# A hybrid decoder step on one core: 64-column chunk-loop weights, spread samples, the two projections one after the other

## The chip, the cores and the metric

One Trainium2 chip, and of it one core with its engines: TensorE (PE; its weight loads are listed as PEld), VectorE (DVE), ScalarE (ACT), GpSimd (POOL) and SyncE (SP), which issues most transfers. The metric is the device time of one execution in microseconds. A kernel's time is the median of its runs.

## The reference

One trunk layer on 512 new tokens of a prompt and 8 single tokens of other sequences, 520 columns in all, of width 2048. A shared RMS norm feeds one wide input projection. From it come a recurrent branch (RWKV-7, 16 heads of 64, with a state of 64 x 64 per head) and a convolution branch (31 taps, a layer norm), each with a gate and a projection to 2048. Two sigmoid gates merge them; an output projection, a per-layer embedding with its own gate, and a final RMS norm follow.

```python
def step(S, inp):
    r_t, w_t, k_t, v_t, a_t, b_t = inp
    sa = jnp.einsum('bhij,bhj->bhi', S, a_t)
    S = S * w_t[:, :, None, :] + sa[..., None] * b_t[:, :, None, :] + v_t[..., None] * k_t[:, :, None, :]
    return S, jnp.einsum('bhij,bhj->bhi', S, r_t)
...
o = ((o - mu) * lax.rsqrt(var + GN_EPS)).reshape(Bn, T, D_A) * lnx_g + lnx_b
...
y_a = jnp.einsum('btc,cd->btd', (o * jax.nn.silu(gate_a.astype(f32))).astype(dt), w_proj_a)
...
cb = jax.nn.silu(cf) * jax.nn.silu(gate_b.astype(f32))
y_b = jnp.einsum('btc,cd->btd', cb.astype(dt), w_proj_b)
m = jax.nn.sigmoid(ga) * y_a + jax.nn.sigmoid(gb) * y_b
h = x + jnp.einsum('btd,de->bte', m, w_out)
```

## The kernel before

The activations lie with channels on the 128 partitions and the 520 tokens along the row. Every large product is done in three passes on split operands: each weight block is split into a high and a low part (`wh` on ScalarE, `wl` on VectorE, both from `split`), the activations likewise, and `step` (L153) issues the six multiplications of one 128 x 128 weight block, three passes by two halves of 260 columns, all recorded as L165. `gemm` (L169) calls `step` 8 or 16 times for one output tile, and after each step calls `tick`.

`tick` (L143) is what interleaves the work. All small work is written as Python generators; each step of a large product advances every generator by one, and `yield n` makes a generator skip n steps. So the `yield` numbers set how many large products stand between two pieces of small work in TensorE's queue, whose order is the order of the program. The queues of the other engines are put in order by the scheduler of the compiler, from the same dependences; each engine runs its queue strictly in order. There are 2224 steps in all.

The main loop (in `rest`'s neighbour at the end of the first stage) runs eight rounds p, one for each pair of heads, with nine products of 16 steps each: k, r, v, the first gate, two for the convolution's gated input, its gate and two of the 32 merge gates, 144 steps a round. Beside it run generators:

- `wkv` (L358): the recurrent branch of round p, one round behind. It makes decays and keys, the column sums `bv` (two multiplications at L257/L258, a few steps after `yield 8`), and the chunk matrices (L446). A 32-row triangular inverse follows on VectorE, a multiplication `tm` and a reduction `ti` (L484) per row, in chunk form for eight chunks of 64 tokens. Then come the transposes of the values (L526) and keys (L538), and the chunk loop (L546 to L574): for each chunk a product with the state columns `suv` (L549), the mask product with `nbr` of the chunk before (L551), a copy `xs`, the product with the inverse `ttb` (L556), copies of its result into `suv` (one on VectorE L557, one on ScalarE L558, and `xu` on POOL L561), the product that updates the state (L564), and on VectorE the update of `suv` (L568) and `sf` (L571). Between these three places are `ly` steps, 4 in most rounds, and 7 in the last. The outputs go through a group norm on VectorE, then, 16 steps later, eight pairs of 64 x 64 transposes (L595, L596), a scale and shift `og`, and two multiplications on POOL.
- `conv` (L621): 30 multiply-adds on VectorE, three steps apart.
- `samples` and `sample` (L658, L678): the single tokens' state update, eight blocks, each four multiplications on POOL and three multiplications or sums and two reductions on VectorE of 128 x 512. They start 12 steps into the last round's generator `rest`.
- `lnorm` (L715): the convolution's layer norm, from `csum`, with the tiles read back from memory; `reload` (L769) brings the recurrent branch's output back as `ya`.

When the rounds and the remaining merge gates are done, the generators are drained, `yb` is split, and for each of 16 output tiles the two projections follow each other, `gemm(8, ya)` and `gemm(8, yb)`, each multiplied by its gate. The output product and the per-layer gate follow; `finish` (L904) does the final norm for each half of the tokens, with multiplications on POOL and VectorE named by `ON_POOL` and written out in `GROUPS`.

## Time and profile before

| | |
|---|---|
| median of 3 runs | 1880.88 us |
| lowest, highest | 1878.25, 1882.21 us |
| profiled execution | 1881.83 us |
| its span | 1880.0 us |
| mean granted clock of TensorE | 0.979 |
| busy: TensorE, VectorE, ScalarE, POOL | 97%, 68%, 41%, 21% |
| moved by transfers | 211.97 MB, mean 113 GB/s |

How to read it: a row of a timeline is start, duration, engine, line, operation, output<-inputs, shape and count; durations of neighbouring matrix products overlap, so that the cost of one is the distance between two starts. A row of the table of waits names the waiting instruction, what released it, the sum, the number and the longest. A granted clock of 0.5 means that TensorE runs at half rate. The rows themselves stand in the prediction.

### The profile page before, as it was taken

To read this page: it belongs to the slowest core of one execution; us is meant where nothing else is said; L and a number is where in the kernel's file an instruction comes from. 1 tells how busy PE (TensorE), PEld (TensorE's weight loads), DVE (VectorE), ACT (ScalarE), POOL (GpSimd) and SP (SyncE) were. 2 spreads that over 40 slices of the span, in tenths; PEclk is the share of its full clock that TensorE was granted. 3 is DMA by queue.
4 is the path that set the end of the run, shared out by engine and by line. 5 is a ranking of instruction groups with operands and counts; after the bars stand their busy time and mean duration, and the time that the engine had idled before them with its cause. 6 is when DMAs were issued, how large, how long until landed. Compare 5 with 4: busy or idle time off the path is not lost.

```text
span 1880.0 us, 37810 instructions
## 1 busy us (share of the span) xinstructions
PE 1823.0 (97%) x15352; PEld 1782.9 (95%) x15352; DVE 1276.0 (68%) x2337; ACT 771.7 (41%) x1478; POOL 397.7 (21%) x514
## 2 busy tenths in 40 slices
PE   9999999999999999999999999999999999999995
PEld 8998998999999999999999999999999999999995
DVE  6679897697797877977977885495433333334457
ACT  6734335336345354363363332464222222243343
POOL 1212214123213213222231372030111000011103
PEclk9999998999999999999999999999999999999998
DMA  7242332432332323323323343456444433252232
GB/s 229 81 117 72 103 100 69 94 106 81 101 102 83 99 88 98 101 86 88 112 76 94 124 153 120 146 165 201 136 136 136 136 118 96 90 192 95 95 103 91
DMA packets 116367, 211.97 MB, mean 113 GB/s; under 512 B 47312, under 2 KB 55632, under 8 KB 116192
## 3 DMA queue, kind: packets, MB, share of 16 engines
q1 hardware_dynamic: 114592, 207.95, 35.9%
q8 instruction: 120, 1.97, 0.4%
q10 hardware_dynamic: 1600, 1.60, 0.3%
q14 instruction: 55, 0.45, 0.1%
HBM read 184.43 MB, written 25.08 MB: 111 GB/s over the span
## 4 chain that ended last, share of the span: by engine, by line
PE 69%; DVE 19%; issue 4%; ACT 3%; POOL 3%; DMA 1%; SPq 0%; DVEq 0%; POOLq 0%; ACTq 0%
PE mm L165 62%; DVE tm L78 5%; DVE wl L78 4%; DVE ti L484 3%; DVE c L643 2%; PE aux L596 1%; PE aux L165 1%; PE aux L446 1%; PE aux L549 1%; ACT wh L81 1%; DVE p L78 1%; PE aux L595 1%; POOL ar L78 1%; PE aux L564 1%; DVE sq L394 1%
## 5 line engine op out<-in xcount | busy, mean ns | idle before, releaser
L165 PE MATMUL mm<-xh,wh 128*128 128x260 f32 x2784 | 593.3, 295 | 0.9 <-ACT xh L219 0.5
L81 ACT ACTIVATE wh<-w 128x512 fp32r<-128x512 f32 (+1 forms) x541 | 338.5, 627 | 621.0 <-PE mm L165 532.2
L78 DVE TENSOR_TENSOR wl<-w,wh 128x512 fp32r<-128x512 f32 (+1 forms) x541 | 386.8, 717 | 280.3 <-ACT wh L81 276.5
L165 PE MATMUL mm<-xh,wl 128*128 128x260 f32 x2784 | 569.4, 286 | 4.8 <-DVE wl L78 4.8
L165 PE MATMUL mm<-xl,wh 128*128 128x260 f32 x2784 | 568.9, 286 | 0.3 <-DVE xl L220 0.3
L165 PEld LDWEIGHTS mm<-xh,wh 128*128 128x128 f32 x2784 | 437.0, 193 | 9.4 <-ACT wh L81 1.1
L165 PEld LDWEIGHTS mm<-xh,wl 128*128 128x128 f32 x2784 | 436.5, 192 | 5.5 <-DVE wl L78 5.4
L165 PEld LDWEIGHTS mm<-xl,wh 128*128 128x128 f32 x2784 | 437.2, 192 | 0.6 <-DVE xl L220 0.5
L165 PE MATMUL mm<-hi,wl 128*128 128x260 f32 x1600 | 333.4, 283 | 3.1 <-DVE wl L78 3.1
L165 PE MATMUL mm<-hi,wh 128*128 128x260 f32 x1600 | 333.3, 283 | 0.0
L165 PE MATMUL mm<-lo,wh 128*128 128x260 f32 x1600 | 332.6, 283 | 0.0
L165 PEld LDWEIGHTS mm<-hi,wl 128*128 128x128 f32 x1600 | 251.0, 189 | 3.3 <-DVE wl L78 3.3
L165 PEld LDWEIGHTS mm<-hi,wh 128*128 128x128 f32 x1600 | 252.1, 189 | 0.1
L165 PEld LDWEIGHTS mm<-lo,wh 128*128 128x128 f32 x1600 | 251.9, 189 | 0.0
L643 DVE SCALAR_TENSOR_TENSOR c<-u,prm,c 128x482 f32<-128x482 f32 (+14 forms) x240 | 188.9, 787 | 3.8
L561 POOL COPY xu<-suv 64x64 f32<-64x64 f32 x128 | 51.4, 402 | 280.8 <-DVE suv L557 271.6
L78 DVE TENSOR_TENSOR tm<-ti,ni 128x16 f32<-128x16 f32 (+30 forms) x248 | 106.5, 429 | 6.0
L78 POOL TENSOR_TENSOR sq<-hi,lo 128x520 f32<-128x520 f32 (+1 forms) x20 | 24.4, 1224 | 337.5 <-DVE one L875 184.0
L78 DVE TENSOR_TENSOR p<-mm,rs 128x520 f32<-128x520 f32 x78 | 54.1, 693 | 48.0 <-PE mm L165 47.8
L484 DVE TENSOR_REDUCE ti<-tm 128x8 f32<-128x16 f32 (+30 forms) x248 | 72.8, 293 | 6.1
L573 ACT ACTIVATE o<-aux 64x64 f32<-64x64 f32 x128 | 28.0, 219 | 92.2 <-DVE sf L571 91.3
L78 POOL TENSOR_TENSOR s<-s,s 128x520 f32<-128x520 f32 x16 | 25.4, 1587 | 171.7 <-DVE s L78 138.8
(243 smaller groups left out, 1774.3 us busy)
## 6 DMA issues: line engine op xcount, KB each, us to landing
w<-in_win SPq DMA_DIRECT2D x170, 512.0 KB, 3.8
w<-in_wout SPq DMA_DIRECT2D x32, 512.0 KB, 3.8
w<-in_wpg SPq DMA_DIRECT2D x24, 512.0 KB, 3.6
w<-in_wpa SPq DMA_DIRECT2D x16, 512.0 KB, 3.6
w<-in_wpb SPq DMA_DIRECT2D x16, 512.0 KB, 3.7
wx<-in_wpg SPq DMA_DIRECT2D x32, 256.0 KB, 4.1
x<-in_xT SPq DMA_DIRECT2D x16, 260.5 KB, 6.8
sga_d<-p SPq DMA_DIRECT2D x16, 260.0 KB, 2.3
```

The lines of the kernel that those rows point to most:

```text
L78: eng.tensor_tensor(out, x, y, op=op)
L81: behind.append(act(hi, x, AF.Copy))
L165: nc.tensor.matmul(o[h], lhsT=w[:, used[0] % 4, :], rhs=x[:, h * HF:(h + 1) * HF], start=(k == 0 and i == 0), stop=(k == nk - 1 and i == 2))
L394: vec.reciprocal(rn[:, h:h + 130], rn[:, h:h + 130])
L446: nc.tensor.matmul(os[h][:, c, :], lhsT=bk[half(h), c0 + c].rearrange("p a t -> p (a t)"), rhs=ar[h][half(h), c0 + c].rearrange("p a t -> ...
L484: last = vec.tensor_reduce(ti[:, :, t], tm[:, :, :t + 1], axis=AX.X, op=ALU.add)
L549: nc.tensor.matmul(x[:, h, :], lhsT=ar[h][:, c].rearrange("p a t -> p (a t)"), rhs=suv[:, h, c, :], start=True, stop=True)
L561: gps.tensor_copy(xu[half(h)], suv[half(h), h, c, :])
L564: nc.tensor.matmul(x[half(h), 3, :], lhsT=bkt[:, c, h * 64:h * 64 + 64], rhs=suv[:, h, c, :], start=True, stop=True)
L573: act(o1[half(1 - h), c, :], x[half(1 - h), h, :], AF.Copy)
L595: nc.tensor.transpose(ot[a0, c, :], o1[a1, c, :], ident[a1, a1])
L643: vec.scalar_tensor_tensor(c[:, d:NPR], u[:, 0:NPR - d], cw[:, k:k + 1], c[:, d:NPR], op0=ALU.mult, op1=ALU.add)
```

## The change

Five parts. First, the chunk loop. Each of the two heads' products uses its own 64 weight columns, so that the two heads' results land in their own halves: one pair for `x`, one pair that opens the accumulation of the output `oc`, and, after the state update, a pair with `nbr` that closes it. The products with `nbr` of the chunk before, the copies `xu` on POOL and the separate output `o1` with its two copies per chunk fall away; both copies of `suv` are on ScalarE, and `xs` is one copy. Second, the group norm's last multiplication becomes four of 64 x 4 x 64, laid out so that four full 128 x 128 transposes do for the sixteen small ones, 22 steps after the loop instead of 16. Third, other `yield` numbers: `bv`, the values and keys before the chunk loop, the last `conv`, the samples, the layer norm. Fourth, all 16 tiles of the first projection come ahead of the 16 of the second; the half-finished tiles are written back to the buffer of the gate and read again; the layer norm ends beside the first projection and makes `yb` itself. Fifth, in the tail, smaller groups and fewer multiplications on POOL for the first half.

```diff
-GROUPS = ([range(4 * _g, 4 * _g + 4) for _g in range(4)],
+GROUPS = ([range(2 * _g, 2 * _g + 2) for _g in range(8)],
...
-ON_POOL = ((1, 2, 3, 5, 6, 7, 9, 10, 11, 13, 14, 15), (12, 13, 14, 15))
+ON_POOL = ((1, 5, 9, 13), (12, 13, 14, 15))
...
-        for j in range(KD):
-            seq += [a["wpa"][j], a["wpb"][j]]
+        seq += [a["wpa"][j] for j in range(KD)] + [a["wpb"][j] for j in range(KD)]
...
             bv = gt("bv")
-            yield 8
+            yield 8 if p > 1 else 18
...
-                    tt(vec, nbr[s, c0:c0 + 4, i:i + 64], o[s, :, i:i + 64], mk(s, 64, 64), ALU.mult)
+                    tt(vec, nbr[s, c0:c0 + 4, h * 64:h * 64 + 64], o[s, :, i:i + 64], mk(s, 64, 64), ALU.mult)
...
-            yield 4
+            yield 6
...
-            yield 5
+            yield 7
...
                 for h in range(2):
-                    nc.tensor.matmul(x[:, h, :], lhsT=ar[h][:, c].rearrange("p a t -> p (a t)"), rhs=suv[:, h, c, :], start=True, stop=True)
-                if c:
-                    nc.tensor.matmul(oc[:, c - 1, :], lhsT=nbr[:, c - 1, :], rhs=xu, start=True, stop=True)
+                    nc.tensor.matmul(x[half(h), 0, :], lhsT=ar[h][:, c, h, :], rhs=suv[:, h, c, :], start=True, stop=True)
+                for h in range(2):
+                    nc.tensor.matmul(oc[half(h), c, :], lhsT=ar[h][:, c, 1 - h, :], rhs=suv[:, h, c, :], start=True, stop=False)
                 xs = kq.tile([P, 64], F32, name="xs", bufs=2)
-                act(xs[0:64], x[0:64, 0, :], AF.Copy)
-                act(xs[64:128], x[64:128, 1, :], AF.Copy)
+                act(xs, x[:, 0, :], AF.Copy)
                 yield ly
                 nc.tensor.matmul(x[:, 2, :], lhsT=ttb[:, c, :], rhs=xs, start=True, stop=True)
-                vec.tensor_copy(suv[0:64, 0, c, :], x[0:64, 2, :])
-                act(suv[64:128, 1, c, :], x[64:128, 2, :], AF.Copy)
-                xu = kq.tile([P, 64], F32, name="xu", bufs=2)
                 for h in range(2):
-                    gps.tensor_copy(xu[half(h)], suv[half(h), h, c, :])
+                    act(suv[half(h), h, c, :], x[half(h), 2, :], AF.Copy)
                 yield ly
                 for h in range(2):
                     nc.tensor.matmul(x[half(h), 3, :], lhsT=bkt[:, c, h * 64:h * 64 + 64], rhs=suv[:, h, c, :], start=True, stop=True)
+                for h in range(2):
+                    nc.tensor.matmul(oc[half(h), c, :], lhsT=nbr[:, c, h * 64:h * 64 + 64], rhs=suv[:, h, c, :], start=False, stop=True)
...
-                for h in range(2):
-                    act(o1[half(1 - h), c, :], x[half(1 - h), h, :], AF.Copy)
...
-            tt(vec, o1, o1, oc, ALU.add)
...
-            tt(vec, o1, o1, bc(m[:, 1]), ALU.mult)
-            yield 16
-            ot = aux().rearrange("p (c x) -> p c x", x=64)
-            a0, a1 = half(0), half(1)
-            for c in range(NCH):
-                nc.tensor.transpose(ot[a0, c, :], o1[a1, c, :], ident[a1, a1])
-                nc.tensor.matmul(ot[a1, c, :], lhsT=o1[a0, c, :], rhs=ident[a0, a0], start=True, stop=True)
+            on = gt("on")[:, :NPR].rearrange("p (c x) -> p c x", x=P)
+            for h in range(2):
+                for e in range(2):
+                    tt(vec, on[half(e), :, h * 64:h * 64 + 64], o1[half(h), e::2, :],
+                       m[half(h), 1, e::2].unsqueeze(2).to_broadcast([64, 4, 64]), ALU.mult)
+            yield 22
+            ot = aux()
+            for c in range(4):
+                nc.tensor.transpose(ot[:, c * P:(c + 1) * P], on[:, c, :], ident)
...
-                yield 3
+                yield 3 if i < 7 else 5
...
-            yield 6
             tt(gps, t1, s0, bc8(1), ALU.mult)
+            yield 3
             tt(gps, s0, s0, bc8(0), ALU.mult)
+            yield 3
             tt(gps, t2, sv[:, 5, i0:i0 + 8].unsqueeze(2).to_broadcast([P, 8, 64]), bc8(3), ALU.mult)
-            yield 3
             vec.tensor_reduce(sa, t1, axis=AX.X, op=ALU.add)
+            yield 2
             tt(vec, t1, sa.unsqueeze(2).to_broadcast([P, 8, 64]), bc8(2), ALU.mult)
+            yield 2
             tt(vec, t1, t1, t2, ALU.add)
+            yield 2
             tt(vec, s0, s0, t1, ALU.add)
             dma(out=a["wkv_s"][:, i0:i0 + 8, :], in_=s0)
+            yield 1
             tt(gps, t2, s0, bc8(4), ALU.mult)
             yield 3
...
-            vec.reciprocal(rl, rl)
-            yield 7
+            for h in range(0, T, 130):
+                vec.reciprocal(rl[:, h:h + 130], rl[:, h:h + 130])
+                yield 2
+            while not flag["merged"]:
+                yield 1
...
+                    yb.append(hl(xp, c1, "x"))
...
+        flag["merged"] = True
+        while len(ya) < 8:
+            tick()
+
+        for j in range(KD):
+            s1 = gt("s1")
+            dma(out=s1, in_=sga_d[j])
+            tt(vec, v2(s1), gemm(8, ya), v2(s1), ALU.mult)
+            dma(out=sga_d[j], in_=s1)
         drain()
-        yb = [hl(xp, cbs[i], "x") for i in range(8)]
...
-            tt(vec, v2(s1), gemm(8, ya), v2(s1), ALU.mult)
             tt(vec, v2(s2), gemm(8, yb), v2(s2), ALU.mult)
...
-                yield 3 * (1 - h)
+                yield 5 * (1 - h)
...
-            start(finish(h, sq, 8 * (1 - h)))
+            start(finish(h, sq, 12 * (1 - h)))
```

Lines of the changed kernel up to the chunk loop bear numbers one lower (L164 for L165). TensorE's order around the first products of a chunk, before:

```order
L165 MATMUL mm<-xh,wl 128x260 x2
L165 MATMUL mm<-xh,wh 128x260 x2
L165 MATMUL mm<-xl,wh 128x260 x2
L165 MATMUL mm<-xh,wl 128x260 x2
L549 MATMUL aux<-suv,ar_10851 128x64
L549 MATMUL aux<-suv,ar_10852 128x64
L551 MATMUL oc<-xu,nbr_797 128x64
L165 MATMUL mm<-xh,wh 128x260 x2
```

and in the changed kernel, at a chunk's first products:

```order
L164 MATMUL mm<-xl,wh 128x260 x2
L164 MATMUL mm<-xh,wl 128x260 x2
L547 MATMUL aux<-suv,ar_10674 64x64
L547 MATMUL aux<-suv,ar_10675 64x64
L549 MATMUL oc<-suv,ar_10674 64x64
L549 MATMUL oc<-suv,ar_10675 64x64
L164 MATMUL mm<-xh,wh 128x260 x2
L164 MATMUL mm<-xl,wh 128x260 x2
```

The product with `nbr` has moved to the chunk's state update, and two pairs of 64 columns stand where two 128-wide products stood.

VectorE's order in round 6 at the update of chunk 6 (L568; L564 in the changed kernel), in the middle of the inverse loop of the next round (`tm`, the number behind it the row of the inverse), before:

```order
L78 TENSOR_TENSOR tm<-ti,ni 128x8x23
L568 SCALAR_TENSOR_TENSOR suv<-sf,epl,aux 64x64
L484 TENSOR_REDUCE ti<-tm 128x8
L568 SCALAR_TENSOR_TENSOR suv<-sf,epl,aux 64x64
L78 TENSOR_TENSOR tm<-ti,ni 128x8x24
L571 SCALAR_TENSOR_TENSOR sf<-sf,epl,aux 128x64
```

and in the changed kernel:

```order
L78 TENSOR_TENSOR tm<-ti,ni 128x8x27
L78 TENSOR_TENSOR p<-mm,rs 128x520
L483 TENSOR_REDUCE ti<-tm 128x8
L564 SCALAR_TENSOR_TENSOR suv<-sf,epl,aux 64x64
L78 TENSOR_TENSOR tm<-ti,ni 128x8x28
L564 SCALAR_TENSOR_TENSOR suv<-sf,epl,aux 64x64
L483 TENSOR_REDUCE ti<-tm 128x8
```

The update has moved four rows of the inverse down the queue, and the multiplication `p` of a large product stands ahead of it.

VectorE's order in round 7 at the update of chunk 0, where the samples' work (`t`, `s`, `sa`, `oso`) is near, before:

```order
L557 COPY suv<-aux 64x64
L78 TENSOR_TENSOR wl<-w,wh 128x512 x2
L568 SCALAR_TENSOR_TENSOR suv<-sf,epl,aux 64x64 x2
L571 SCALAR_TENSOR_TENSOR sf<-sf,epl,aux 128x64
L668 TENSOR_REDUCE sa<-t_13979 128x8
L78 TENSOR_TENSOR wl<-w,wh 128x512
L78 TENSOR_TENSOR t_13979<-sa,sv 128x512
```

and in the changed kernel:

```order
L78 TENSOR_TENSOR wl<-w,wh 128x512
L78 TENSOR_TENSOR s_13917<-s_13917,t_14254 128x512
L638 SCALAR_TENSOR_TENSOR c<-u,prm,c 128x511
L674 TENSOR_REDUCE oso<-t_14255 128x8
L663 TENSOR_REDUCE sa<-t_14410 128x8
L78 TENSOR_TENSOR wl<-w,wh 128x512
L78 TENSOR_TENSOR t_14410<-sa,sv 128x512
L564 SCALAR_TENSOR_TENSOR suv<-sf,epl,aux 64x64 x2
L567 SCALAR_TENSOR_TENSOR sf<-sf,epl,aux 128x64
```

Before, the update stood behind one sample's work and ahead of the other seven's; now it stands behind that of five samples and the start of the sixth. `oso<-t_14255` reads the 28th of the 32 multiplications of the samples in POOL's queue.

More of the change, by code (lines that the diff above doesn't have):

```diff
@@ L354, in body @@
         d11 = kq.tile([P, NCH, 32], F32, name="d11")
-        flag = {"inv": None, "done": -1, "loop": -1, "conv": 0, "yp": None}
+        flag = {"inv": None, "done": -1, "loop": -1, "conv": 0, "yp": None, "merged": False}
         def wkv(p, k, box):
@@ L526, in wkv @@
                 nc.tensor.transpose(o[:, w, :], v[:, w * P:(w + 1) * P], ident)
-            for h in range(2):
-                for e in range(2):
+            for e in range(2):
+                for h in range(2):
                     act(suv[half(1 - h), h, e::2], o[half(e), :, h * 64:h * 64 + 64], AF.Copy)
@@ L571, in wkv @@
                 vec.scalar_tensor_tensor(sf, s0, epl[:, c:c + 1], x[:, 3, :], op0=ALU.mult, op1=ALU.add)
-                for h in range(2):
-                    act(o1[half(1 - h), c, :], x[half(1 - h), h, :], AF.Copy)
                 yield ly
-            nc.tensor.matmul(oc[:, NCH - 1, :], lhsT=nbr[:, NCH - 1, :], rhs=xu, start=True, stop=True)
             flag["done"] = p
@@ L579, in wkv @@
             bc = lambda x: x.unsqueeze(2).to_broadcast([P, NCH, 64])
-            tt(vec, o1, o1, oc, ALU.add)
+            o1 = gt("o1")[:, :NPR].rearrange("p (c x) -> p c x", x=64)
             m = kq.tile([P, 2, NCH], F32, name="m")
-            vec.tensor_reduce(m[:, 0], o1, axis=AX.X, op=ALU.add)
+            vec.tensor_reduce(m[:, 0], oc, axis=AX.X, op=ALU.add)
             gps.tensor_scalar(m[:, 0], m[:, 0], 1.0 / 64, 0.0, op0=ALU.mult, op1=ALU.add)
-            tt(vec, o1, o1, bc(m[:, 0]), ALU.subtract)
+            tt(vec, o1, oc, bc(m[:, 0]), ALU.subtract)
             sq = gt("sq")[:, :NPR].rearrange("p (c x) -> p c x", x=64)
@@ L589, in wkv @@
             vec.reciprocal(m[:, 1], m[:, 1])
-            tt(vec, o1, o1, bc(m[:, 1]), ALU.mult)
-            yield 16
-            ot = aux().rearrange("p (c x) -> p c x", x=64)
-            a0, a1 = half(0), half(1)
-            for c in range(NCH):
-                nc.tensor.transpose(ot[a0, c, :], o1[a1, c, :], ident[a1, a1])
-                nc.tensor.matmul(ot[a1, c, :], lhsT=o1[a0, c, :], rhs=ident[a0, a0], start=True, stop=True)
+            on = gt("on")[:, :NPR].rearrange("p (c x) -> p c x", x=P)
+            for h in range(2):
+                for e in range(2):
+                    tt(vec, on[half(e), :, h * 64:h * 64 + 64], o1[half(h), e::2, :],
[4 more added lines that the diff above has]
+                nc.tensor.transpose(ot[:, c * P:(c + 1) * P], on[:, c, :], ident)
             og = gt("og")[:, :NPR]
             sl = box["sl"]
-            act(og, ot.rearrange("p c x -> p (c x)"), AF.Identity, scale=col(O_LG, p), bias=col(O_LB, p))
+            act(og, ot, AF.Identity, scale=col(O_LG, p), bias=col(O_LB, p))
             tt(gps, og, og, bv[:, :NPR], ALU.add)
@@ L710, in samples @@
             dma(out=oa_d[:, :, NPR:].rearrange("a p b -> p a b"), in_=oa)
-        cbs = []
+        cbs, yb = [], []
         def lnorm():
@@ L736, in lnorm @@
                     cbs.append(x)
-                yield 2
+                yield 4
                 if vs is None:
@@ L758, in lnorm @@
                     act(s, c, AF.Sigmoid)
-                    yield 2
+                    yield 3
                 if prev:
@@ L763, in lnorm @@
                     tt(gps, c1, c1, g1, ALU.mult)
+                    yield 3
+                    yb.append(hl(xp, c1, "x"))
                 prev = (c, g, s)
-                yield 1
+                yield 3
         ya = []
```

1 line of the change is left out of this document (removed).

## The prediction

> **What bounds the kernel now.** I read the page first: who is busy, and what the chain that ended last runs through.
>
> ```profile
> PE 1823.0 (97%) x15352; PEld 1782.9 (95%) x15352; DVE 1276.0 (68%) x2337; ACT 771.7 (41%) x1478; POOL 397.7 (21%) x514
> ```
>
> The critical chain, in order of time, then shows where TensorE is never interrupted.
>
> ```profile
> 1247.43 586.37 PE mm L165 x4871
> ```
>
> TensorE is the bound. From 1247 to 1834 us it runs without a wait, so nothing moved there (merges, both projections, the output product) can gain, only lose. What can be gained lies in three places: TensorE's own small instructions, its waits, and stretches at a lower clock. The table of waits of TensorE comes next, over the span and then for 460 to 1100 us alone.
>
> ```profile
> PE aux L564 <- ACT suv L558: 10.4, 10, 3.7
> PE mm L165 <- DVE wl L78: 7.9, 4, 3.1
> PE aux L549 <- DVE suv L568: 7.6, 8, 3.5
> PE aux L595 <- DVE o L78: 4.1, 5, 1.0
> PE aux L257 <- ACT hi L81: 1.9, 1, 1.9
> PE aux L258 <- DVE lo L78: 1.8, 1, 1.8
> ```
>
> ```profile
> PE aux L564 <- ACT suv L558: 5.5, 7, 1.0
> PE aux L556 <- ACT xs L554: 1.8, 3, 0.6
> ```
>
> Columns: microseconds in all, times, longest. Most waits belong to the chunk loop (L549, L556, L564) and to the group norm's transposes (L595). The two longest, 3.7 and 3.5 us, are in round 7, where the samples run.
>
> The clock is read from windows laid around its dips; first those that begin in or just behind a group of transposes L595/L596 (columns: stretch, length, TensorE busy, count, granted clock, DMA share, GB/s).
>
> ```profile
> 306.00:316.00 10.00, 10.00 (x56) 0.66 0.34 97
> 415.00:422.00 7.00, 7.00 (x69) 0.76 0.28 76
> 661.00:671.00 10.00, 9.52 (x51) 0.66 0.30 109
> 792.00:801.00 9.00, 7.99 (x49) 0.81 0.25 94
> 922.00:931.00 9.00, 8.05 (x51) 0.81 0.31 99
> 1053.00:1064.00 11.00, 10.53 (x58) 0.69 0.43 128
> 1246.00:1252.00 6.00, 6.00 (x37) 0.72 0.66 223
> ```
>
> Length times what the clock lacks to 1 is 3.4, 1.7, 3.4, 1.7, 1.7, 3.4 and 1.7 us, 17.0 in all. Two of the seven stretches are fully busy, so it isn't a wait that lowers the clock there.
>
> **The change, part by part.** The sum goes against the profiled execution: 1881.8 us, of which 1880.0 span. It lies 0.9 us above the median of 1880.9.
>
> *Transposes.* The timeline of one round's group, at full clock first, at half clock from the sixth pair on:
>
> ```profile
> 661.48 0.24 PE L595 MATMUL aux<-cst,o 64*64 64x64 f32 x1 [0.69 <-DVE o L78]
> 661.91 0.24 PE L595 MATMUL aux<-cst,o 64*64 64x64 f32 x1
> ...
> 664.22 0.31 PE L595 MATMUL aux<-cst,o 64*64 64x64 f32 x1
> 664.86 0.31 PE L595 MATMUL aux<-cst,o 64*64 64x64 f32 x1
> 665.50 0.80 PE L165 MATMUL mm<-xh,wh 128*128 128x260 f32 x2
> ```
>
> One pair costs 0.43 us start to start (661.48 to 661.91), eight pairs 3.44, eight rounds 27.5. The four full transposes that replace them are of the kind at L538:
>
> ```profile
> 557.97 1.04 PE L538 MATMUL aux<-cst,bk 128*128 128x128 f32 x8
> 558.76 0.48 PE L165 MATMUL mm<-xh,wh 128*128 128x260 f32 x2
> ```
>
> Eight in 0.79 us, so four cost 0.4 and eight rounds 3.2. **−24.3**, with little doubt. The layout that this needs is four small multiplications on VectorE in place of one; they come 22 steps, some 16 us, ahead of the transposes instead of 16 steps, so the wait L595 on `o` goes: **−4.1** (−4.1 to 0).
>
> *Clock.* The seven dips follow groups that keep a quarter of the array busy for 3.4 us. With 0.4 us of full transposes I expect no dip. Of the 17.0 not all is time: a pair takes 0.64 us at the halved clock (664.22 to 664.86) against 0.43, 1.5 times and not twice. I take **−14** (−17 to 0). The Trainium skill, "TensorE: Matmul & The Clock Gate", Part 4: PE-mode transpose, says that a transpose doesn't count as a busy TensorE; by that it is the transposing, not the small tile, that lowers the clock. This trace has the eight transposes of L538 at 557.97 with 128-wide products following at the usual pace, which speaks for a short group being harmless.
>
> *Chunk loop.* The timeline around two of a chunk's places:
>
> ```profile
> 607.83 0.56 PE L549 MATMUL aux<-suv,ar 128*128 128x64 f32 x4
> 608.42 0.49 PE L165 MATMUL mm<-xh,wh 128*128 128x260 f32 x2
> ...
> 614.01 0.40 PE L165 MATMUL mm<-xl,wh 128*128 128x260 f32 x2
> 614.25 0.40 PE L165 MATMUL mm<-xh,wl 128*128 128x260 f32 x2
> 614.58 0.34 PE L564 MATMUL aux<-suv,bkt 128*64 128x64 f32 x4
> 614.84 0.51 PE L165 MATMUL mm<-xh,wh 128*128 128x260 f32 x2
> ```
>
> Two large products take 0.24 us (614.01 to 614.25), but 0.33 with the entry into 64-column weights (614.25 to 614.58): 0.09 for the entry, 0.26 for the pair. A 128-wide pair with its nbr product costs 0.59. Before, a chunk pays 0.59 + 0.35 here, 0.94. After, two pairs at each of two places: each place 0.09 + 0.26 and, for the pair that needs no change back, about 0.23, so 0.58, both 1.16. That is 0.22 more per chunk, 14.1 for 64: **+14**. If the entry price were paid for every pair it would be +26; if the halves of a new pair did not run side by side, see the rivals. The Trainium skill, "TensorEngine Tiling (Array Packing)", Key Properties, says that changing the tiling mode drains TensorE: a rule against this change, which doubles such places from 64 to 128. The trace agrees with it; 64 more entries at the 0.09 above are 6 us, already within the +14.
>
> *State updates in rounds 2 to 6.* The chunk loop comes four steps later (yields 6 and 7 for 4 and 5), while VectorE works through the inverse loop. The order puts the update of chunk 6 behind the 27th row of the inverse and a `p`; before, it stood at the 23rd. The rows three rounds earlier, TensorE's and then VectorE's:
>
> ```profile
> 637.80 0.56 PE L549 MATMUL aux<-suv,ar 128*128 128x64 f32 x4
> ...
> 641.35 0.33 PE L556 MATMUL aux<-xs,ttb 128*128 128x64 f32 x2
> ```
>
> ```profile
> 642.04 0.55 DVE L78 TENSOR_TENSOR tm<-ti,ni 128x216 f32<-128x216 f32 x1
> 642.62 0.38 DVE L484 TENSOR_REDUCE ti<-tm 128x8 f32<-128x216 f32 x1
> 643.03 1.17 DVE L78 TENSOR_TENSOR tm<-ti,ni 128x224 f32<-128x224 f32 x1
> ```
>
> Chunk 7 began at 637.80; four steps later is where its L556 stood, 641.35. By then both halves of the update must be done. VectorE ends the 27th row at 642.6 less what is no longer ahead of it (some 1.7 us of updates, copy and `p`), 640.9; `p`, a reduction, half an update, the 28th row and the other half follow, 2.3 to 2.8 us, so 643.2 to 643.7. TensorE waits about 2 us, five times 10, and in two of five rounds I allow a dip of 1.7: 13.4. What it replaces is 5.5 + 1.8 = 7.3, the late copy of `suv` on VectorE and `xs`, which do go: both copies are on ScalarE now and POOL's `xu` is gone. **+6** (−7 to +17).
>
> *Round 7, samples.* POOL's queue is in order. All 32 sample multiplications now stand behind `og` of round 6, which follows the transposes, ten steps later than here:
>
> ```profile
> 1053.47 0.24 PE L595 MATMUL aux<-cst,o 64*64 64x64 f32 x1 [0.72 <-DVE o L78]
> 1102.20 0.55 PE L549 MATMUL aux<-suv,ar 128*128 128x64 f32 x4
> ```
>
> Ten steps are sixty products at the 0.12 above, 7.2 us: the transposes come at about 1061, `og` and its two multiplications on POOL follow, so the first sample's stands at some 1065 to 1067. VectorE's update of chunk 0 stands, in the new order, behind a reduction that needs the 28th of these. The groups by line of 1090 to 1140 us give POOL's price beside a busy VectorE:
>
> ```profile
> L78 POOL TENSOR_TENSOR t<-s,sv 128x512 f32<-128x512 f32 x13 | 20.5, 1580 | 6.0 <-DVE s L78 4.3 <-DMA s<-in_swkv 1.6
> ```
>
> 28 by 1.58 is 44 us: 1109 to 1111, plus 3 us for the rows on VectorE up to the update, 1112 to 1114. Chunk 1 began at 1102.20; it comes four steps later, 2.9 us, and the 3.6 us of old transposes ahead of it are gone: about 1101.5. TensorE waits some 11 to 13 us there or for a `wl` queued behind the same rows, and with two dips of 1.7 loses about 15. What it lost here before, with the dips:
>
> ```profile
> 1118.00:1146.00 28.00, 20.74 (x134) 0.76 0.30 92
> ```
>
> 28 − 20.74 of missing busy time is 7.3, and of it 7.2 are the 3.7 and 3.5 of the waits; the two dips add about 4, so 11. **+4** (−11 if POOL keeps up, +20 if the two engines take turns throughout).
>
> *First rounds.* `bv` waits 18 steps instead of 8 in rounds 0 and 1; the 1.9 + 1.8 us at L257 and L258 go, and about 1.2 of the dip in this window:
>
> ```profile
> 92.00:102.00 10.00, 6.28 (x38) 0.83 0.20 52
> ```
>
> **−4.9** (−5 to 0). The preparation of the chunks moves ten steps with it, which gives VectorE more time in the crowded stretch up to 200 us: **−2** (−7 to +5).
>
> *Projections and the layer norm.* Sixteen reads and writes of 260 KB more, hidden behind 128 steps of products; the layer norm's 81 steps fit beside them, and one VectorE multiplication per product is as before. If the cover were missing, TensorE would wait for `yb` at the second projection: **0** (0 to +5). *Tail.* The 3.1 us at L165 for a `wl` lies there, behind multiplications on VectorE and POOL; smaller groups with more steps between spread them: **−1** (−4 to +3).
>
> Sum: −24.3 − 4.1 − 14 + 14 + 6 + 4 − 4.9 − 2 + 0 − 1 = −26.3. 1881.8 − 26.3 = 1855.5, against the median 1854.6; I say **1855**.
>
> **The rivals.** *The waits go entirely.* The updates come in time in rounds 2 to 6 and the samples keep up: −7 and −11 instead of +6 and +4, 28 less: 1827. For it: the yields of the samples are spread over 17 steps instead of 13. Against it: the queue order, which gathers them all ahead of chunk 1. Between the two, half of it, 1841.
>
> *The clock dips stay.* What lowers the clock may be the stop of the large products, with the transposes counted as idle: 1855 + 14 = 1869. The rule of the skill on transposes says so. Against it: 0.4 us is far shorter than the 3.4 us of the old groups.
>
> *Slower: the state updates become the bound.* One mechanism: VectorE's queue in order, with the update behind other work. At +17 in rounds 2 to 6, +20 in round 7, and the same in rounds 0 and 1 (+5 for −2), it is 34 more than I take: 1889. It decides from a lateness of about 5 us a round. For it: the order rows; against it: VectorE is 68% busy and the old lateness was at most 1.0 us in 460 to 1100.
>
> *Slower: the new 64-column pairs run one half behind the other.* An unpaired pair costs 4 passes of 0.11, 0.45 instead of 0.23; three pairs a chunk, 64 chunks: +42, 1897. Against it: L564 is the same form, and its four records take 0.26 us.
>
> *It doesn't do what it says:* the samples stay bunched. That is in the forecast already.
>
> **How the numbers follow.** Forecast 0.48 (1847 to 1863); waits gone wholly or half 0.24 (1827 to 1845); dips stay 0.13 (1865 to 1873); updates bound 0.10 (1875 to 1895); unpaired halves 0.05. The range leaves out the lowest end of the second case and most of the last two: 1832 to 1880. A measurement of this kernel can tell about 0.2%, 3.8 us, from no change. Faster takes the first three cases and a little of the fourth, 0.86; same 0.04; slower 0.10.
>
> **What would show it.** Right: L591 groups of 0.4 us with no half-clock stretch behind, clock above 0.985; two pairs in about 0.5 us at L547/L549; one wait of over 5 us near chunk 1 of round 7; waits of about 2 us at chunk 7 of rounds 2 to 6. Wrong: dips behind L591; pairs of 0.45; waits above 4 us a round in the chunk loop; any wait between 1250 and 1830.

## The result and the profile after

The changed kernel takes 1871.58 us, median of 5 runs (1868.31 to 1873.20); the kernel before, beside it, 1880.88 (1878.25 to 1883.80). The ratio is 0.9947, 95% interval 0.9931 to 0.9963: 9.3 us faster, where 26 were forecast. The profiled execution has a span of 1871.3 us, 8.7 less than before.

The page first, engine by engine:

```profile
PE 1793.5 (96%) x15576; PEld 1747.9 (93%) x15576; DVE 1261.6 (67%) x2300; ACT 746.8 (40%) x1356; POOL 339.5 (18%) x378
```

TensorE is busy 29.5 us less, and yet the span is only 8.7 us shorter: the rest has become waiting. The waits of TensorE over the span:

```profile
PE mm L164 <- DVE wl L78: 23.3, 13, 3.7
PE aux L547 <- DVE suv L564: 16.9, 17, 5.2
...
PE mm L164 <- DVE s L78: 3.1, 3, 1.7
...
PE aux L558 <- ACT suv L555: 2.1, 1, 2.1
...
PE mm L164 <- ACT sg L760: 1.7, 1, 1.7
```

The split weight `wl` was 7.9 us and the state update `suv` 7.6; both have grown, and the first projection waits, for `s` and `sg`, which it did not. The mean granted clock is 0.984. What was won is seen in the windows laid around the new transposes, and in the timeline of one group:

```profile
534.00:540.00 6.00, 6.00 (x78) 1.00 0.34 124
662.00:672.00 10.00, 10.00 (x136) 1.00 0.46 154
788.00:797.00 9.00, 9.00 (x102) 1.00 0.34 119
1044.00:1054.00 10.00, 10.00 (x137) 1.00 0.69 195
1240.00:1246.00 6.00, 6.00 (x53) 1.00 0.65 211
1066.00:1108.00 42.00, 23.89 (x161) 0.81 0.32 103
```

```profile
661.34 0.60 PE L591 MATMUL aux<-cst,on 128*128 128x128 f32 x4
661.69 0.49 PE L164 MATMUL mm<-xh,wh 128*128 128x260 f32 x2
```

Behind the transposes the clock is 1.00 everywhere, and a group costs 0.35 us. The last window is the loss: in round 7, TensorE is busy for 23.89 of 42 us, at a clock of 0.81.

Since the large products stand in the same sequence in both kernels, the two traces can be laid against each other product by product. The start of a step's first large product, after less before, shows where time is won and lost:

| step | place | after less before, us |
|---|---|---|
| 94 | start of round 0's column sums | -0.9 |
| 290 | round 1, before the first transposes | -10.1 |
| 361 | round 1, in the inverse | -24.5 |
| 380 | the same, once VectorE has caught up | -9.3 |
| 1181 | end of round 6 | -22.9 |
| 1229 | round 7, after chunk 0 | +2.0 |
| 1342 | samples done in both | -11.9 |
| 1424 | start of the projections | -15.1 |
| 1480 | within the first projection | -9.2 |
| 2190 | last products | -9.2 |

The kernel is 22.9 us ahead at the end of round 6. It loses 24.9 us around chunk 0 of round 7, regains 13.9 (mostly where the kernel before waited), and loses 5.9 in the first projection.

### The profile page after: what moved, and what is told of

Its sections match the earlier page's. It is cut to its first block, busy times and chain, and to the rows that moved or that the text cites. A ratio compares the mean times of both kernels' runs of the same rounds, so it can differ in the third digit from the quotient of the medians.

```text
span 1871.3 us, 37932 instructions
## 1 busy us (share of the span) xinstructions
PE 1793.5 (96%) x15576; PEld 1747.9 (93%) x15576; DVE 1261.6 (67%) x2300; ACT 746.8 (40%) x1356; POOL 339.5 (18%) x378
## 4 chain that ended last, share of the span: by engine, by line
PE 59%; DVE 23%; issue 7%; ACT 6%; POOL 3%; DMA 2%; SPq 0%; DVEq 0%; POOLq 0%; ACTq 0%
PE mm L164 54%; DVE c L638 5%; DVE wl L78 4%; DVE tm L78 3%; DVE ti L483 2%; DVE sq L393 1%; PE aux L445 1%; PE aux L164 1%; ACT wh L81 1%; DVE p L78 1%; DMA y<-oa_d 1%; DVE t L78 1%; POOL a L78 1%; DVE lo L78 1%; DVE suv L564 1%
## 5 line engine op out<-in xcount | busy, mean ns | idle before, releaser
L164 PE MATMUL mm<-xh,wh 128*128 128x260 f32 x2784 | 588.8, 293 | 0.1
L164 PE MATMUL mm<-xh,wl 128*128 128x260 f32 x2784 | 567.1, 285 | 20.3 <-DVE wl L78 20.3
L78 DVE TENSOR_TENSOR wl<-w,wh 128x512 fp32r<-128x512 f32 (+1 forms) x541 | 382.3, 710 | 298.4 <-ACT wh L81 294.0
L164 PE MATMUL mm<-xl,wh 128*128 128x260 f32 x2784 | 565.3, 284 | 0.0
L164 PEld LDWEIGHTS mm<-xh,wl 128*128 128x128 f32 x2784 | 433.0, 191 | 22.8 <-DVE wl L78 22.8
L164 PEld LDWEIGHTS mm<-xh,wh 128*128 128x128 f32 x2784 | 432.4, 191 | 11.9 <-ACT wh L81 0.6
L164 PEld LDWEIGHTS mm<-xl,wh 128*128 128x128 f32 x2784 | 433.2, 190 | 0.3 <-DVE xl L219 0.2
L164 PE MATMUL mm<-hi,wh 128*128 128x260 f32 x1600 | 334.2, 284 | 4.9 <-DVE s L78 3.1
L164 PE MATMUL mm<-hi,wl 128*128 128x260 f32 x1600 | 334.2, 284 | 3.0 <-DVE wl L78 3.0
L164 PE MATMUL mm<-lo,wh 128*128 128x260 f32 x1600 | 333.1, 283 | 0.0
L164 PEld LDWEIGHTS mm<-hi,wh 128*128 128x128 f32 x1600 | 252.6, 189 | 5.7 <-ACT sg L760 4.9
L164 PEld LDWEIGHTS mm<-hi,wl 128*128 128x128 f32 x1600 | 251.4, 189 | 3.5 <-DVE wl L78 3.5
L164 PEld LDWEIGHTS mm<-lo,wh 128*128 128x128 f32 x1600 | 252.4, 189 | 0.0
L638 DVE SCALAR_TENSOR_TENSOR c<-u,prm,c 128x482 f32<-128x482 f32 (+14 forms) x240 | 195.8, 816 | 4.1
L78 POOL TENSOR_TENSOR sq<-hi,lo 128x520 f32<-128x520 f32 (+1 forms) x20 | 24.3, 1220 | 337.8 <-DVE one L885 184.0
L564 DVE SCALAR_TENSOR_TENSOR suv<-sf,epl,aux 64x64 f32<-64x64 f32 x112 | 31.0, 277 | 26.3 <-PE aux L558 17.3
L78 DVE TENSOR_TENSOR s<-mm,s 128x520 f32<-128x520 f32 x32 | 22.3, 698 | 35.5 <-PE mm L164 35.5
```

What stands on the lines that cost most here:

```text
L78: eng.tensor_tensor(out, x, y, op=op)
L164: nc.tensor.matmul(o[h], lhsT=w[:, used[0] % 4, :], rhs=x[:, h * HF:(h + 1) * HF], start=(k == 0 and i == 0), stop=(k == nk - 1 and i == 2))
L564: vec.scalar_tensor_tensor(suv[s, h, c + 1, :], sf[s], epl[s, c:c + 1], x[s, 3, :], op0=ALU.mult, op1=ALU.add)
L638: vec.scalar_tensor_tensor(c[:, d:NPR], u[:, 0:NPR - d], cw[:, k:k + 1], c[:, d:NPR], op0=ALU.mult, op1=ALU.add)
```

## The experiments

Each run is compared with the kernel before on the same chip (its medians there lay between 1881.2 and 1882.5 us).

### The samples, the projections, the transposes and the yields ahead of the chunk loop

*Old yields for the samples*, in the changed kernel:

```diff
             sa = kp.tile([P, 8], F32, name="sa", bufs=2)
+            yield 6
             tt(gps, t1, s0, bc8(1), ALU.mult)
-            yield 3
             tt(gps, s0, s0, bc8(0), ALU.mult)
-            yield 3
...
```

> The changed kernel with the samples' old yields. Theory A (POOL's queue lost the xu copies that held the samples back until each chunk's suv was there, so they run in one burst whatever the yields): the burst and its 18 us of TensorE waits around chunk 0 and 1 of round 7 stay, time within 4 us of the changed kernel's 1871.6. Rival B (the new yields place the samples badly): the loss falls back to the old 11 us, time about 1860.

1864.82 us (1864.26 to 1866.64), ratio 0.9911 (0.9897 to 0.9924): 6.8 faster than the change. It is neither theory's number, but round 7 decides between them. The waits of TensorE from 1045 to 1110 us:

```profile
PE mm L164 <- DVE wl L78: 13.9, 6, 4.8
PE aux L547 <- DVE suv L564: 5.1, 1, 5.1
```

The burst is as large as in the change (12.9 and 5.2 from 1050 to 1110), so the new yields do not spread the samples. What went is the loss in the first projection: 1.5 us instead of 5.9 by the comparison of steps, since the samples and with them the layer norm end earlier.

*Old projections and layer norm*, in the changed kernel:

```diff
-        seq += [a["wpa"][j] for j in range(KD)] + [a["wpb"][j] for j in range(KD)]
+        for j in range(KD):
+            seq += [a["wpa"][j], a["wpb"][j]]
...
-        for j in range(KD):
-            s1 = gt("s1")
-            dma(out=s1, in_=sga_d[j])
-            tt(vec, v2(s1), gemm(8, ya), v2(s1), ALU.mult)
-            dma(out=sga_d[j], in_=s1)
         drain()
+        yb = [hl(xp, cbs[i], "x") for i in range(8)]
...
```

> The changed kernel with the projections tile by tile in turn and the layer norm as before. Theory A (layer norm and first projection share VectorE, ScalarE and POOL; the 5 us of waits at 1277 to 1300 us are theirs alone): the waits go, 5.9 us faster, about 1866. Rival B (the work only moves and is waited for elsewhere, at the old place or at the second projection): within 2 us of 1871.6.

1882.99 us (1878.94 to 1884.38), ratio 1.0002 (0.9994 to 1.0011): 11.4 slower than the change. Both theories fall: the waits do not go but grow. From 1180 to 1310 us the layer norm's column sums (L257, L258) and the projection wait for what is late:

```profile
PE aux L257 <- ACT hi L81: 3.7, 1, 3.7
PE mm L165 <- DVE p L78: 2.7, 1, 2.7
PE mm L165 <- DVE wl L78: 2.5, 1, 2.5
```

By the comparison of steps 2.7 us of the difference arise around chunk 0 of round 7, and 8.7 behind step 1342, where the layer norm and the projections are. So the split projection is cover for a layer norm that the change itself has made late.

*The transposes alone*, in the kernel before, 16 steps behind the loop:

```diff
-            tt(vec, o1, o1, bc(m[:, 1]), ALU.mult)
+            on = gt("on")[:, :NPR].rearrange("p (c x) -> p c x", x=P)
+            for h in range(2):
+                for e in range(2):
+                    tt(vec, on[half(e), :, h * 64:h * 64 + 64], o1[half(1 - h), e::2, :],
+                       m[half(1 - h), 1, e::2].unsqueeze(2).to_broadcast([64, 4, 64]), ALU.mult)
             yield 16
...
-            for c in range(NCH):
-                nc.tensor.transpose(ot[a0, c, :], o1[a1, c, :], ident[a1, a1])
-                nc.tensor.matmul(ot[a1, c, :], lhsT=o1[a0, c, :], rhs=ident[a0, a0], start=True, stop=True)
+            for c in range(4):
+                nc.tensor.transpose(ot[:, c * P:(c + 1) * P], on[:, c, :], ident)
```

> The kernel before with the full transposes alone (16 steps after the loop, as before). Theory A (the transposes and the clock dips behind them are worth what was forecast, and the rest of the change gave it back): 30 to 40 us faster than before, 1841 to 1851, no half-clock stretch behind the transposes. Rival B (the dips come from elsewhere, or the four small multiplications are late and TensorE waits for them): 8 to 20 us faster, 1861 to 1873.

1869.55 us (1866.73 to 1872.56), ratio 0.9938 (0.9924 to 0.9951): Rival B's size, by its second reason. From 460 to 1100 us TensorE waits

```profile
PE aux L598 <- DVE on L78: 10.1, 5, 2.2
```

for the four multiplications. No half-clock stretch stands behind a group unless such a wait stood ahead of it.

*The same with 22 steps*, `yield 22` for `yield 16`:

> The kernel before with the full transposes alone, 22 steps behind the loop instead of 16. Theory A (with 16 steps the four multiplications came 2 us late in five rounds; 22 steps cover them): the 10 us of waits at the transposes go, 8 to 11 us faster than with 16 steps, 1859 to 1862. Rival B (VectorE is late there anyway, so the wait only moves to the chunk loop of the next round): within 3 us of 1869.6.

1859.56 us (1857.71 to 1861.48), ratio 0.9884 (0.9870 to 0.9897): Theory A, 10 us. The clock behind two of the groups:

```profile
658.00:668.00 10.00, 10.00 (x111) 1.00 0.48 156
911.00:921.00 10.00, 10.00 (x112) 1.00 0.43 134
```

So the transposes with their 22 steps are worth 21.6 us alone, more than twice the whole change, though not the 42.4 of the forecast. By the comparison of steps, from 8 steps ahead of an old group to 16 behind it, the eight groups win 6.5, 4.6, 4.0, 6.8, 5.8, 5.7, 6.9 and 4.7 us, 45.0 in all. But 23.0 are given back: 5.3 ahead of the first group, nearly nothing around the second, 2.3 to 2.6 a round between the third group and the seventh, 3.6 in round 7 and 4.2 behind the last. TensorE has waits that have grown; over the span these three stood at 0.4 us, nothing and 10.4 in the kernel before:

```profile
PE aux L515 <- ACT sig L382: 4.9, 1, 4.9
PE aux L549 <- ACT suv L529: 4.2, 6, 1.1
PE aux L564 <- ACT suv L558: 15.4, 11, 6.1
```

The first lies ahead of the first group and the second in the chunk loops; of the third, 8.7 us are in round 7, where it was 3.7.

*Old yields 4 and 5 ahead of the chunk loop*, in the changed kernel, `yield 4` for `yield 6` and `yield 5` for `yield 7`:

> The changed kernel with the old yields 4 and 5 ahead of the chunk loop. Theory A (four steps later put chunk 6's update behind more rows of the inverse; that is the 1.7 us wait at chunk 7 of rounds 2 to 6): waits at L547 fall by 8 to 10 us, about 1863. Rival B (the old place has waits of its own at chunks 1 and 2 and at the bkt products): within 3 us of 1871.6 or slower.

1872.57 us (1872.04 to 1873.02), ratio 0.9950 (0.9938 to 0.9963): Rival B. From 460 to 1040 us the waits at L547 for the update fall from 9.2 to 0.7 us, and these stand in their place:

```profile
PE aux L257 <- DVE lo L78: 5.0, 4, 1.5
PE oc L549 <- ACT suv L528: 3.7, 4, 0.9
PE aux L547 <- ACT suv L528: 2.4, 4, 0.8
```

### Holding the samples back

In the kernel with the samples' old yields, the chunk loop of round 7 makes a one-column copy on POOL of what each of its three places has produced; every sample's first multiplication is queued behind the latest of these copies, one sample for two places:

```diff
+            def mark(n, t):
+                if p == 7:
+                    t0 = kq.tile([P, 1], F32, name="mk", bufs=2)
+                    flag["mark"] = (n, gps.tensor_copy(t0, t[:, :1]))
...
+                mark(3 * c, xs)
                 yield ly
...
+            while flag["mark"][0] < 2 * (i0 // 8) - 2:
+                yield 1
...
-            tt(gps, t1, s0, bc8(1), ALU.mult)
+            with tc.issue_after(flag["mark"][1].ins) if flag["mark"][1] else ExitStack():
+                tt(gps, t1, s0, bc8(1), ALU.mult)
```

> The changed kernel with the samples' old yields, and each sample held back on POOL behind a one-column copy of what the chunk loop has just made, two places of the loop for each sample. Theory A (the burst of samples ahead of chunk 0 and 1 is what TensorE waits for): the waits of 1066 to 1106 us, 18 us with 6 at half clock, fall below 6, time 1847 to 1855. Rival B (VectorE has more work than fits between the chunks of round 7 wherever it stands): the waits spread over chunks 0 to 4, time 1860 to 1868.

1840.27 us (1838.88 to 1843.37), ratio 0.9787 (0.9773 to 0.9800): beyond Theory A. Round 7 has no wait of TensorE at all, in two windows:

```profile
1045.00:1110.00 65.00, 65.00 (x615) 1.00 0.50 156
1110.00:1200.00 90.00, 90.00 (x786) 1.00 0.46 142
```

*The changed kernel with nothing but the holding*, its new yields for the samples kept:

> The changed kernel with the samples held and nothing else altered, its new yields for the samples kept. If the place of the samples alone is the loss: 1838 to 1843, as with the old yields (1840.3). If the longer yields cost by themselves, since the samples end later and the layer norm with them: 3 to 6 us slower than that, 1843 to 1846.

1846.78 us (1845.54 to 1846.99), ratio 0.9808 (0.9794 to 0.9821). The holding alone is worth 24.8 us, and the longer yields cost 6.5 on top (5.2 if each kernel is taken against the kernel before on its own chip): the first projection loses 8.0 us by the comparison of steps, against 1.5 with the old yields.

*The kernel before with the transposes (22 steps) and held samples:*

> The kernel before with the full transposes 22 steps behind the loop and the samples held as in the run of 1840; the chunk loop, the first rounds, the projections and the tail stay old. Theory A (the new chunk loop's products cost TensorE nothing more and nothing less, and what the rest of the change is worth lies in the first rounds): the 1859.6 less the 11 us that the old samples cost, 1848 to 1851. Rival B (the new chunk loop is what lets the samples go without waits, since it took the copies off VectorE and POOL): waits in round 7 stay, 1855 to 1860.

1845.45 us (1843.88 to 1846.04), ratio 0.9805 (0.9791 to 0.9818): slightly beyond Theory A. The old samples cost 14.1 us, more than the 11 of their waits and dips.

*Yields 5 and 6 ahead of the chunk loop*, with held samples (`yield 5` for `yield 6`, `yield 6` for `yield 7`):

> The kernel with held samples and the yields 5 and 6 ahead of the chunk loop, two steps earlier than in the change, two later than before. Theory A (chunk 7 waits since its update stands behind too many rows of the inverse; two rows fewer go further than two steps earlier cost): the 1.3 + 0.46 us a round at chunk 7 fall, 3 to 8 us faster, 1832 to 1837. Rival B (the wait moves to chunk 1 and the bkt products, as with 4 and 5): within 2 us of 1840.3 or slower.

1830.74 us (1830.08 to 1833.59), ratio 0.9731 (0.9718 to 0.9744), 51 us faster than before and 41 faster than the change: the fastest of all, and just beyond Theory A's range. The waits for the update from 460 to 1040 us, first with 6 and 7, then with 5 and 6:

```profile
PE aux L552 <- DVE suv L571: 9.3, 13, 1.3
```

```profile
PE aux L552 <- DVE suv L571: 2.2, 3, 1.2
```

### What lowered the clock

Four kernels add work behind each round's transposes: the first repeats the four transposes, and the others write tiles that nobody reads.

```diff
-            for c in range(4):
+            for c in range(32):
+                c %= 4
                 nc.tensor.transpose(ot[:, c * P:(c + 1) * P], on[:, c, :], ident)
```

> The changed kernel with the four full transposes of each round done eight times over, 3.2 us a round, the length of the old group. Theory A (the small tiles lowered the clock): no half-clock stretch behind the group, 8 times 2.8, 22 us slower than the changed kernel, about 1894. Rival B (transposes count as idle whatever their size): half-clock stretches behind most groups, 22 and 10 to 17 us more, 1904 to 1911.

One run, 1889.11 us: nearer Theory A's 1894 than the 1904 to 1911 of Rival B, and the clock agrees with it. The clock behind a group of 3.65 us of full transposes:

```profile
664.09 3.65 PE L592 MATMUL aux<-cst,on 128*128 128x128 f32 x32
```

```profile
664.00:674.00 10.00, 10.00 (x114) 1.00 0.31 105
1054.00:1064.00 10.00, 10.00 (x113) 1.00 0.50 157
```

The Trainium skill, "TensorE: Matmul & The Clock Gate", Part 4: PE-mode transpose, says that a transpose doesn't count as a busy TensorE in the same way. For full transposes this trace doesn't bear that out: 3.65 us of them left the clock at 1.00.

```diff
+            od = aux()
+            for c in range(16):
+                nc.tensor.matmul(od[0:64, c % 8 * 64:c % 8 * 64 + 64], lhsT=on[0:64, c % 4, 0:64], rhs=ident[0:64, 0:64], start=True, stop=True)
```

> The changed kernel with 16 additional plain products of 64 x 64 behind each round's transposes, 3.4 us a round, into a tile that nobody reads. Theory A (small tiles lower the clock): half-clock stretches behind the groups, 27 us and 10 to 17 us more, 1908 to 1915. Rival B (transposes do, plain products don't): none, about 1899.

One run, 1885.87 us, and no dip in rounds 2 to 6 behind a group. It tells less than planned: the products took 2.07 us, not 3.4. The next two are on the kernel with held samples:

```diff
+            od = aux().rearrange("p (c x) -> p c x", x=64)
+            a0, a1 = half(0), half(1)
+            for c in range(NCH):
+                nc.tensor.transpose(od[a0, c, :], on[a1, c % 4, 64:128], ident[a1, a1])
+                nc.tensor.matmul(od[a1, c, :], lhsT=on[a0, c % 4, 0:64], rhs=ident[a0, a0], start=True, stop=True)
```

> The kernel with held samples, and behind each round's four full transposes one more group of the old make, eight pairs of a 64 x 64 transpose and a 64 x 64 product, 3.4 us, into a tile that nobody reads. If the old make of the group lowers the clock: half-clock stretches behind most of the eight groups, 27.5 us and 10 to 17 more, 1878 to 1885. If the dips of the kernel before came from something else at that place (the wait ahead of the group): none, about 1868.

One run, 1870.91 us, short of the 1878 to 1885; the clock decides between the two cases. The old make brings the dips back, behind six of the eight groups, with no wait ahead of them (a seventh stands behind the first group, but there the clock had been at half just before):

```profile
667.15 0.60 PE L599 MATMUL aux<-cst,on 128*128 128x128 f32 x4
667.68 0.24 PE L603 MATMUL aux<-cst,on 64*64 64x64 f32 x1
667.86 0.32 PE L604 MATMUL aux<-cst,on 64*64 64x64 f32 x2
668.11 0.24 PE L603 MATMUL aux<-cst,on 64*64 64x64 f32 x1
...
670.68 0.28 PE L603 MATMUL aux<-cst,on 64*64 64x64 f32 x1
```

```profile
667.00:677.00 10.00, 10.00 (x67) 0.83 0.40 118
799.00:809.00 10.00, 10.00 (x67) 0.83 0.38 130
930.00:940.00 10.00, 10.00 (x67) 0.83 0.38 112
```

*Small transposes without products between them* (24 of the first line, in place of the eight pairs):

> The kernel with held samples, and behind the four full transposes 24 more transposes of 64 x 64, without products between them, into a tile that nobody reads. If small transposes are what lowers the clock: half-clock stretches behind most groups. If only the alternation of transposes and products, or the wait, does: none. At the old price of 0.17 us each, 4 us a round, 33 us: about 1873 without dips, 1883 to 1890 with.

One run, 1857.20 us, no dip at the groups. But it too was short: 24 in 1.53 us, 0.064 each, where one in the old group took 0.17.

```profile
662.40 1.53 PE L603 MATMUL aux<-cst,on 64*64 64x64 f32 x24
```

So it is shown that the old make of the group lowers the clock and that full transposes of the same length don't. Whether small tiles alone would, over 3.4 us, stays open: the tiles slow down 3.0 us behind the first small one (667.68 to 670.68), in the kernel before 2.2 (661.48 to 663.63), and the groups of 2.07 and 1.53 us had ended by then.

### One part undone, or one part alone

*Old projections and layer norm on the fastest kernel* (the edit as above):

> The kernel of 1830.7 (held samples, yields 5 and 6) with the projections tile by tile in turn and the layer norm as before. If the split projection earns something only because the samples of the change end late: within 3 us of 1830.7. If it covers the layer norm in any case: 8 to 12 us slower, 1839 to 1843, as when the same part was undone alone.

1832.81 us (1832.53 to 1834.46), ratio 0.9743 (0.9730 to 0.9756) against 0.9731 (0.9718 to 0.9744): 2.1 slower, not told apart from no difference. With samples that end in time the split projection earns next to nothing, against 11.4 us in the change.

*Old yield 8 in rounds 0 and 1 on the fastest kernel:*

```diff
-            yield 8 if p > 1 else 18
+            yield 8
```

> The kernel of 1830.7 with the old yield 8 ahead of the column sums in rounds 0 and 1. If the term of the forecast holds (-4.9, all of it in the first 130 us): 4 to 6 us slower, 1835 to 1837. If VectorE bounds the first rounds, so that what is won at 100 us is lost again by 390 us: within 2 us of 1830.7.

1841.57 us (1840.95 to 1843.60), ratio 0.9789 (0.9776 to 0.9803): 10.8 slower, twice the forecast term and outside both cases, and none of it is lost later.

*Old tail on the fastest kernel* (`GROUPS`, `ON_POOL`, 3 for 5 and 8 for 12):

> The kernel of 1830.7 with the old tail (groups of four, twelve multiplications on POOL, the old waits). By the forecast's -1 for the tail: 1 us slower, 1831 to 1833. By the first trace, where the tail lost 1.4 us: 1 to 2 faster.

1832.83 us (1830.75 to 1834.83), ratio 0.9741 (0.9727 to 0.9755) against 0.9731 (0.9718 to 0.9744): 2.1 slower, not told apart from no difference.

*The new chunk loop alone*, with yields 5 and 6, on the kernel of 1845.45:

> The kernel of 1845.5 (before, with full transposes and held samples) with the new chunk loop and yields 5 and 6, and nothing else of the change. If the forecast's price for the 64-column pairs were right: 14 us slower from TensorE's own time, 1855 to 1860. If the second pair of a place costs 0.12 us and the loop comes out even, with fewer copies on three engines: 1836 to 1845.

1844.90 us (1839.07 to 1846.87), ratio 0.9796 (0.9779 to 0.9813): even, as the second case had it, within runs that spread over 7.8 us. The timeline of one of a chunk's two places in the changed kernel tells why:

```profile
598.12 0.40 PE L164 MATMUL mm<-xh,wl 128*128 128x260 f32 x2
598.45 0.34 PE L558 MATMUL aux<-suv,bkt 128*64 128x64 f32 x4
598.62 0.29 PE L560 MATMUL oc<-suv,nbr 128*64 128x64 f32 x4
598.83 0.51 PE L164 MATMUL mm<-xh,wh 128*128 128x260 f32 x2
```

From 598.45 to 598.83 two pairs take 0.38 us, against 0.26 for one. The second pair costs 0.12, not 0.23; the entry is 0.33 less 0.24, as before. The other place, at 601.90, takes 0.39 for its two pairs. Two places a chunk then cost 2 x 0.47 = 0.94, what they cost before.

*The same without the holding:*

> The kernel of 1844.9 (before, with the full transposes and the new chunk loop) without the holding of the samples; their yields are the old ones. If the new chunk loop by itself lets the scheduler put the samples ahead of chunk 0, as the order of this kernel has it: 20 to 28 us slower, 1865 to 1873. If the burst needs the other parts of the change: about 14 us slower, as the old order costs, 1857 to 1861.

1863.05 us (1861.09 to 1863.79), ratio 0.9894 (0.9881 to 0.9908): 18 slower, a little short of the first case. In round 7 itself, from step 1181 to 1250, the traces differ by 24.8 us (18.6 lost, where the held kernel wins 6.2). Against that stand 7.0 us ahead of round 7 and 3.8 behind step 1250. In the first 900 us VectorE, ScalarE and POOL have the same operations in the same order in both traces, by name and shape, so the 7.0 are no other order of the scheduler, and their cause stays open; the held kernel's profiled execution is the slowest of its five. So the new chunk loop, with yields 5 and 6, brings the burst, with the samples' old yields and without the rest of the change.

## Why the prediction was wrong

The direction and the range held; the size did not. That the range held is partly luck, since large errors cancel. The parts, as the runs price them (the difference of medians named in each row):

| part | forecast, us | measured, us | from |
|---|---|---|---|
| full transposes, clock, wait for `o` | -42.4 | -21.6 | transposes with 22 steps alone |
| new chunk loop with yields 5 and 6 | +14 | -0.6 | chunk loop alone, held |
| yields 6 and 7 instead of 5 and 6 | +6 | +9.5 | 1840.27 less 1830.74 |
| place of the samples | +4 | +10.7 | 24.8 for the holding, less the 14.1 that the old place cost |
| longer yields of the samples | 0 | +6.5 | 1846.78 less 1840.27 |
| first rounds | -6.9 | -10.8 | old yield 8 |
| projections | 0 | -2.1 | old projections, held |
| tail | -1 | -2.1 | old tail |
| sum | -26.3 | -10.5 | the change: -9.3 |

The rows follow one chain of kernels from before to the change, so that they nearly have to add up; the sum proves no single row. The medians come from several chips, on which the kernel before differs by up to 1.7 us, so a row is good to about 2 us, and the two of -2.1 are not told apart from nothing. The forecast's +6 is for the whole step from yields 4 and 5 to 6 and 7, of which the row before has a part: the two rows together are +20 forecast and +8.9 measured. With the old yields put back into the change, that step alone made no difference (1872.57).

**The step that failed** is the overlap that the term for the transposes takes for granted: "−24.3", "−4.1" and "−14" enter the sum in full, −42.4, as if all that TensorE saves there were time of the kernel. Measured alone, in the kernel before, it is −21.6, a miss of 20.8 us, the largest of the table. The local price was right: 0.43 and 0.35 us measured as forecast, the waits for `o` gone, no dip behind the groups (window rows above), and 45.0 us won around the eight groups. The term gave nothing for what the other engines would take back, and 23.0 us were given back between the groups. The three waits shown with that run have grown by 13.7 of them; in the chunk loops between the third group and the seventh about half of what is given back is not traced to a wait. (Three of the seven half-clock windows of the prediction are fully busy, not two.)

**Round 7** is the second step: the term "+4 (−11 if POOL keeps up, +20 if the two engines take turns throughout)", with its end in the first projection, "0 (0 to +5)", together +17 for +4. The mechanism was the one described. POOL from the samples' first multiplication on, and then VectorE, at the update of chunk 0 in the change:

```profile
1050.09 1.84 POOL L78 TENSOR_TENSOR t<-s,sv 128x512 f32<-128x512 f32 x1 [0.45 <-DMA s<-in_swkv]
...
1077.35 3.33 POOL L78 TENSOR_TENSOR t<-s,sv 128x512 f32<-128x512 f32 x2 [1.22 <-DVE oso L674]
...
1100.11 1.70 POOL L78 TENSOR_TENSOR t<-s,sv 128x512 f32<-128x512 f32 x1 [1.23 <-DVE s L78]
```

```profile
1101.85 0.69 DVE L674 TENSOR_REDUCE oso<-t 128x8 f32<-128x512 f32 x1 [1.15 <-POOL t L78]
...
1105.12 0.58 DVE L564 SCALAR_TENSOR_TENSOR suv<-sf,epl,aux 64x64 f32<-64x64 f32 x2
```

Each waits for the other, and the update stands behind both. The size was off: I took 11 to 13 us of waits, and there were 18.1 (12.9 + 5.2). What was mis-sized is the length of POOL's chain, 28 multiplications at 1.58, 44 us. They are busy for those 44 us, but the chain lasts 51.7, from 1050.1 to 1101.8, with 7.3 us of waits in it, 5.1 for VectorE and 2.2 for a transfer. The chain began 6.2 us behind the transposes, about as forecast, so it came earlier together with what was won ahead of it. Nor did I see the second price of the samples: their yields, which I costed at nothing, moved the layer norm into the projection.

**Chunk loop.** The +14 was mis-sized by the second pair's price: 0.23 stood on no row, and 0.12 was measured. The rival of unpaired halves is refuted by the same rows. This error, 14.6 us, hid much of the other two.

**State updates** were right in kind and place: from 460 to 1040 us the wait is 9.2 us over 13 times, up to 1.3 each, and 8.4 of it is at chunk 7 of rounds 2 to 6, where 10 were expected.

**First rounds.** They won more than forecast, but the waits at the column sums did not go: 2.4 and 3.2 us (L256, L257) stand between 300 and 345 us in the change, with 3.2 more at L445. The change is 24.5 us ahead at step 361, where it still has the first transposes before it, and 9.3 at step 380.

**The other rivals and signs.** The dips that stay are refuted for full transposes; waits brought new ones, 0.81 from 1066 to 1108 us. The updates as the bound came true in round 7 alone, so the kernel did not become slower. That the waits go entirely did not happen in the change; with the samples held they go in round 7, and with yields 5 and 6 besides the time is 1830.7, near that rival's 1827. One sign of being wrong did appear, waits between 1250 and 1830: 4.8 us from 1265 to 1305, in the first projection.

**Why the samples moved.** Neither their yields nor the rest of the change did it, but the new chunk loop, through the scheduler's order. The yields ahead of it are not needed either: with 4 and 5 in the change, 25.8 us are lost around chunk 0 of round 7. Which of the chunk loop's edits gives the scheduler the room was not tried.

## What to carry to other kernels

When code order sets only one engine's queue, a yield or a reordering does not place the work of the others: read the queue's order, and where a burst must be spread, tie it to something that the paced loop produces. Price a saving by where the next engine is late, not by the instructions that go: of 45 us won around the transposes 23 were given back. Price a chain that passes to and fro between two engines with the waits of each for the other, not by the busy time of one. A group of small transposes that alternates with products costs more than its instructions, since the clock falls behind it.

## What was not expected of the hardware

A 64 x 64 transpose takes 0.064 us among its like (24 in 1.53 us) and 0.17 in turn with products (668.11 to 668.28). A second pair of 64-column products adds 0.12 us to a first of 0.26. A stretch of 3.65 us of full 128 x 128 transposes left the granted clock at 1.00, where 3.4 us of alternating small ones took it to 0.83 over ten microseconds.
